# Split-precision matmuls reordered, weight remainders moved to VectorE, router logits transposed, and the mixer's per-head products issued two heads in turn

## The chip, the cores and the metric

The kernel runs on 1 core of one Trainium2 chip, written in Bass with the Tile framework. The metric is the device time of one execution in microseconds (us); a run's time is read from the device, and a profiled execution gives the trace from which every row below is taken. TensorE (PE) multiplies, VectorE (DVE) and GpSimd (POOL) work elementwise, ScalarE (ACT) casts and evaluates functions, SyncE (SP) issues the transfers of weights. Matmul results land in PSUM, which has 8 banks a partition.

## The reference

Two layers on 256 tokens of width 1024. Each layer is a token mixer with three branches (mLSTM with 4 heads, forgetting attention with 8 heads, RWKV7 with 8 heads), then cross-attention to 256 memory tokens, then a feed-forward part (dense SwiGLU in layer 0, a mixture of 8 experts with top 2 in layer 1), each closed by a residual LayerNorm.

```python
def _token_mixer(x, w_in, b_in, ...):
    p = x @ w_in + b_in
    h_a = _mlstm(m_q, m_k, m_v, col('m_i'), col('m_f'))
    ...
    h_b = _forgetting_attention(f_q, f_k, f_v, col('f_f'))
    ...
    y = _rwkv7_scan(r, decay, k, v, kk, kk * a)
    ...
    merged = gates[..., 0, :] * (h_a @ m_up) + gates[..., 1, :] * (h_b @ f_up) + gates[..., 2, :] * (y @ r_up)
    return merged @ w_out, v_own

def _moe(x, router_w, router_b, ex_wgu, ex_wd):
    logits = (x @ router_w).astype(jnp.float32) + router_b
    top_v, top_i = lax.top_k(logits, TOP_K)
    top_w = jax.nn.softmax(top_v, axis=-1)
    comb = jnp.sum(jax.nn.one_hot(top_i, N_EXPERTS, dtype=jnp.float32) * top_w[..., None], axis=-2).astype(x.dtype)
    y = jnp.zeros_like(x)
    for e in range(N_EXPERTS):
        y = y + comb[..., e:e + 1] * _swiglu(x, ex_wgu[e], ex_wd[e])
    return y

def reference(x, mem, ...):
    for l in range(DEPTH):
        mix, v_own = _token_mixer(x, *mixer_params[l], vres)
        x = _post_norm(x, mix, *ln1[l])
        x = _post_norm(x, _cross_attention(x, mem_n, *xattn[l]), *ln2[l])
        f = _swiglu(x, *ffn[l]) if l % 2 == 0 else _moe(x, *ffn[l])
        x = _post_norm(x, f, *ln3[l])
    return x
```

All inputs are fp32, and the results have to be near fp32, which sets how the kernel multiplies.

## The kernel before, in words

**Weights.** All large weights stream from HBM in 912 chunks of 512 KB (128 partitions x 1024). `chunk` (L286) transfers one to `raw` (queue of SP), ACT casts it to `whi` (L295, a rounded fp32r copy), and the remainder `wlo` = `raw` - `whi` is subtracted on DVE (L297). A list called `aside` sends 3 subtractions at the end of each `out_proj` to POOL instead, 15 in all. Activations are split in the same way into a high and a low part (`xh` and `xl`, `hh` and `hl`). `mm3` (L323) then makes one product of three fp32r matmuls at L331: `whi`·`xh`, `whi`·`xl`, `wlo`·`xh`, in that order for each of the `kt` blocks of the contraction.

**Stages.** Each layer runs `attention` (the mixer, L415), an `out_proj` (L389) with a LayerNorm, `cross` (L1056), another `out_proj`, then `dense` (L1120) in layer 0 or `moe` (L1148) in layer 1. Tile's scheduler orders the instructions of each engine by priority and dependence; every engine then runs its list in order, and PSUM tiles come from small rings by tag. In the mixer the rings are `g` (projections `fps`, 2 banks), `r` (RWKV grams and scratch, 2), `a` (scores of all three branches, 2), `p` (1) and `y` (1).

**The mixer.** `_mixer_heads` (L472) goes through a list, ORDER: projections of each branch (`fps`, 24 matmuls of 256 columns for each 128 outputs) in turn with the head work that depends on them; the projections are the filler under the head work, which has long chains through DVE, ACT and POOL.
- `_mlstm` (L653): for each head a decay bias into `mcb`, scores `msc` = K·Q (contraction over 64, so over one half of the rows of the PE array; L669, L670), then `mnm`.
- `_fox` (L709), for two heads at a time: for each head scores `flg` = q·k (64 rows; L718, L721) with the forget bias (`grow`, `cst`) and a causal mask `negts` added by matmuls into the same PSUM tile, softmax, transposes `fpt`, then `fot` = V·P (64 output columns, one column half of the array; L746, L747).
- `_rwkv_pre` (L751): the small products `rzw` and `rza` (64 rows each, L761 and L762) and, in layer 1, `rvp` (32 rows).
- `_rwkv_chain` (L847), called once for heads pairs 0 and 1 (`c0`) and once for 2 and 3 (`c1`): for each head and each of two 128-token blocks a tile `rg` of four 128x128 gram products (64 rows, L860), masked into SBUF by DVE; then an elimination chain of 15 steps through DVE and POOL that ends in the tile `ZX` (POOL, L888), which the PE product `rzz` (L894) reads.

Products with 64 rows or 64 columns use half of the array. They are plain fp32, and one of 256 columns is two records in the trace.

**The router.** `moe` makes logits `elp` (L1195) with 128 tokens of x stationary and the 16 router columns `rwp` moving, then the top 2, their positions and the gather lists with many DVE operations on tiles of 8 to 16 columns (L1200 to L1211); meanwhile POOL splits the tokens into `xth` and `xtl` (L1221). `experts` (L1283) then streams the 672 expert chunks: the big expert of each pair goes through `mm3` into `egu`, the small ones through a block of four matmuls a chunk (L1355).

Of the kernel before, what the change touches and what calls it, by code (L numbers as in the profile page):

```python
# [9 lines left out]
F32 = mybir.dt.float32  # L10
# [9 lines left out]
P = 128  # L20
# [40 lines left out]
ASIDE = 3  # L61
# [160 lines left out]
class Model:  # L222
# [10 lines left out]
    def setup(self, ip):  # L233
# [29 lines left out]
        self.negts = self.cp.tile([P, P], BF, name="negts")  # L263
# [4 lines left out]
        nc.vector.tensor_copy(self.negts, t[:, 2])  # L268
# [17 lines left out]
    def chunk(self, src, kt, n):  # L286

        nc, e = self.nc, kt * n
        pool, nraw = self._turn(0)
        raw = pool.tile([P, 1024], F32, name="raw", tag="raw", bufs=nraw)  # L290
        pool, nparts = self._turn(1)
        hi = pool.tile([P, 1024], F32R, name="whi", tag="whi", bufs=nparts)
        lo = pool.tile([P, 1024], F32R, name="wlo", tag="wlo", bufs=nparts)
        nc.sync.dma_start(raw[:, :e], src)
        nc.scalar.copy(hi[:, :e], raw[:, :e])  # L295
        eng = nc.gpsimd if self.aside and self.aside.pop(0) else nc.vector
        eng.tensor_tensor(lo[:, :e], raw[:, :e], hi[:, :e].bitcast(F32), op=OP.subtract)  # L297
        f = lambda t: t[:, :e].rearrange("p (k n) -> p k n", k=kt)
        return f(hi), f(lo)
# [23 lines left out]
    def mm3(self, ps, wh, wl, xh, xl, kt, w_stat, wsl, xsl, first=True, last=True):  # L323
# [3 lines left out]
        for k in range(kt):  # L327
            for a, b in ((wh, xh), (wh, xl), (wl, xh)):
# [60 lines left out]
    def out_proj(self, W, xs, tail, lname, xh, xl, done=None, mid=None):  # L389
# [15 lines left out]
        self.aside = [False] * (7 - tail) + [True] * ASIDE  # L405
# [247 lines left out]
    def _mlstm(self, l, qk, v1, mo, mh, ml):  # L653
        nc, wk = self.nc, self.wk
        num = wk.tile([P, 2, 4, P + 1], F32, name="mnum", tag="w4", bufs=4)
        for h in range(4):
            j, r = h // 2, slice((h % 2) * 64, (h % 2) * 64 + 64)
            cb = self.ap.tile([P, 384], F32, name="mcb", tag="a")
            sel = self._bcast('selc', h)
            nc.tensor.matmul(cb[:, 0:256], sel, self.Q, start=True, stop=False)  # L660
            nc.tensor.matmul(cb[:, 0:128], self.identb, self.negst, start=False, stop=True)
            nc.tensor.matmul(cb[:, 256:384], sel, self.Q[:, 128:256], start=True, stop=False)
            nc.tensor.matmul(cb[:, 256:384], self.identb, self.negst, start=False, stop=True)
            w = wk.tile([P, 384], F32, name="mw", tag="w15", bufs=2)
            nc.vector.tensor_scalar(w[:, 0:256], cb[:, 0:256], self.qc[:, 0, h:h + 1], 0.0, op0=OP.add, op1=OP.min)
            nc.vector.tensor_scalar(w[:, 256:384], cb[:, 256:384], self.qc[:, 1, h:h + 1], 0.0, op0=OP.add, op1=OP.min)
            nc.scalar.activation(w, w, AF.Exp)
            sc = self.ap.tile([P, 384], F32, name="msc", tag="a")
            nc.tensor.matmul(sc[:, 0:256], qk[r, 2 + j, 0:128], qk[r, j, :], start=True, stop=True)  # L669
            nc.tensor.matmul(sc[:, 256:384], qk[r, 2 + j, 128:256], qk[r, j, 128:256], start=True, stop=True)  # L670
            nc.vector.scalar_tensor_tensor(w, sc, 1.0 / 32.0, w, op0=OP.mult, op1=OP.mult)
            nm = self.ap.tile([P, 2, P + 1], F32, name="mnm", tag="a")
            nc.tensor.matmul(nm[:, 0], w[:, 0:128], v1[:, 0, h], start=True, stop=True)
            nc.tensor.matmul(nm[:, 1], w[:, 128:256], v1[:, 0, h], start=True, stop=False)
            nc.tensor.matmul(nm[:, 1], w[:, 256:384], v1[:, 1, h], start=False, stop=True)
            nc.scalar.copy(num[:, :, h], nm)
# [32 lines left out]
    def _fox(self, l, fq, fk, fv, fh, fl):  # L709
        nc, wk = self.nc, self.wk  # L710
        for j in range(4):
            pts = []
            for hh in range(2):
                h = 2 * j + hh
                r = slice(hh * 64, hh * 64 + 64)
                sel = self._bcast('self', h)
                lg = self.ap.tile([P, 384], F32, name="flg", tag="a")
                nc.tensor.matmul(lg[:, 0:128], fq[r, j, 0:128], fk[r, j, 0:128], start=True, stop=False)  # L718
                nc.tensor.matmul(lg[:, 0:128], sel, self.Q[:, 0:128], start=False, stop=False)
                nc.tensor.matmul(lg[:, 0:128], self.identb, self.negts, start=False, stop=True)  # L720
                nc.tensor.matmul(lg[:, 128:384], fq[r, j, 128:256], fk[r, j, :], start=True, stop=False)  # L721
                nc.tensor.matmul(lg[:, 128:384], sel, self.Q, start=False, stop=False)
                nc.tensor.matmul(lg[:, 256:384], self.identb, self.negts, start=False, stop=True)
# [12 lines left out]
                nc.vector.tensor_scalar(p[:, 128:384], p[:, 128:384], sm[:, 3:4], None, op0=OP.mult)  # L736
                pt = self.ap.tile([P, 384], F32, name="fpt", tag="a")
                for i in range(3):
                    nc.tensor.transpose(pt[:, i * P:(i + 1) * P], p[:, i * P:(i + 1) * P], self.ident)
                ptb = wk.tile([P, 384], F32, name="fptb", bufs=2)  # L740
                nc.scalar.copy(ptb, pt)
                pts.append(ptb)
            ot = self.ap.tile([P, S], F32, name="fot", tag="a")
            for hh in range(2):
                r, d = slice(hh * 64, hh * 64 + 64), slice(j * P + hh * 64, j * P + hh * 64 + 64)
                nc.tensor.matmul(ot[r, :], fv[:, 0, d], pts[hh][:, 0:256], start=True, stop=False)  # L746
                nc.tensor.matmul(ot[r, 128:256], fv[:, 1, d], pts[hh][:, 256:384], start=False, stop=True)  # L747
# [3 lines left out]
    def _rwkv_pre(self, l, j, x, v_first):  # L751
# [8 lines left out]
        za = pp.tile([P, S], F32, name="rza", tag="p")  # L760
# [86 lines left out]
    def _rwkv_chain(self, l, pairs, yfull):  # L847
# [6 lines left out]
        for j, (KR, BX, vt, bon, lm) in pairs:  # L854
            for hh in range(2):
                q = slice(hh * 64, hh * 64 + 64)
                for c in range(2):
                    g = rp.tile([P, 4, P], F32, name="rg", tag="r")
                    for b in range(2):
                        nc.tensor.matmul(g[:, 2 * b:2 * b + 2].rearrange("p a b -> p (a b)"), BX[q, c, b],  # L860
                                         KR[q, c].rearrange("p a b -> p (a b)"), start=True, stop=True)
                    m = self.grams[len(M)]
                    nc.vector.copy_predicated(m, self.keep.rearrange("p a b -> p (a b)"),
                                              g.rearrange("p a b -> p (a b)"))
                    M.append(m.rearrange("p (a b) -> p a b", a=4))
# [282 lines left out]
    def moe(self, l, xh, xl):  # L1148
        tc, nc, A = self.tc, self.nc, self.A
        xt = self.xt  # L1150
        with ExitStack() as ctx:
# [37 lines left out]
            pos = wk.tile([P, 2, NE], F32, name="epos")  # L1189
            pp = tp.tile([P, 5, NE], F32, name="epp", tag="t")  # L1190
            for tt in range(2):
                lp = self.gp.tile([P, 2, NE], F32, name="elp", tag="g")
                for k in range(KD):
                    for part in (xh, xl):
                        nc.tensor.matmul(lp.rearrange("p a b -> p (a b)"), part[:, k, tt * P:(tt + 1) * P],  # L1195
                                         rwp[:, k].rearrange("p a b -> p (a b)"), start=k == 0 and part is xh,
                                         stop=k == KD - 1 and part is xl)
                nc.vector.tensor_tensor(lg[:, tt], lp[:, 0], rb, op=OP.add)
                nc.vector.tensor_tensor(lg[:, tt], lg[:, tt], lp[:, 1], op=OP.add)
                nc.vector.max(mx[:, tt], lg[:, tt])  # L1200
                nc.vector.max_index(ix[:, tt], mx[:, tt], lg[:, tt])
                nc.vector.tensor_copy(ixf[:, tt], ix[:, tt])
# [303 lines left out]
```

## Time and profile before

| what | value |
|---|---|
| runs of the kernel | 2164.92, 2165.76 (median), 2166.17 us |
| profiled execution, its own time | 2165.97 us |
| its span in the trace | 2164.2 us |
| mean granted TensorE clock | 0.987 |
| PE busy | 2082.1 us, 96% of the span, 11726 matmul records |
| DVE, ACT, POOL busy | 1601.9, 1222.3, 227.6 us |
| HBM moved | 532.18 MB, 246 GB/s over the span |

The profiled execution is within 0.21 us of the median of the runs, and 1.8 us of its time lie outside its span. "Busy" counts a matmul from its start to its modelled end, so an engine that is shown as busy may still lose time between starts: pace has to be read from start to start. The stages lie in the span as follows: mixer of layer 0 to about 345 us, mixer of layer 1 from about 700 to 1060 us, last LayerNorm and router 1179 to 1214 us, experts 1214 to 2130 us.

### The profile page before, as it was taken

What the parts mean: (1) busy time and instruction counts of PE and PEld (TensorE: products, weight loads), DVE (VectorE), ACT (ScalarE), POOL (GpSimd) and SP (SyncE); (2) the same over time, 40 slices, a digit from 0 to 9 for tenths busy, and PEclk for the clock granted to TensorE, in tenths of its full rate; (3) what the DMA queues carried; (4) which work ended last, traced back from release to release, by engine and by line L of the source; (5) the groups of instructions that cost most, each with busy time, mean ns of one, the idle gap of its engine ahead of it and who ended that gap; (6) DMA issues with size and microseconds to landing.
All of it is one profiled execution on the core that took longest, in us unless ns stands there. A gap on an engine that the chain in (4) does not pass through costs nothing.

```text
span 2164.2 us, 33290 instructions
## 1 busy us (share of the span) xinstructions
PE 2082.1 (96%) x11726; PEld 1724.1 (80%) x11726; DVE 1601.9 (74%) x2327; ACT 1222.3 (56%) x1723; POOL 227.6 (11%) x332
## 2 busy tenths in 40 slices
PE   7999999999999899999998899999999999999996
PEld 6988898989998788889887777777767767777674
DVE  6776656746555677665675698889888988899887
ACT  5443334544443544332453587777777777777774
POOL 0031142202001113114212100000000000000000
PEclk9999999999999999999999799999999999999998
DMA  5431335645553543133574599999999999999994
GB/s 199 157 120 59 135 123 200 253 151 202 189 185 124 173 152 111 62 104 111 214 263 146 179 366 393 389 363 363 388 388 363 372 386 385 391 354 372 379 393 181
DMA packets 146767, 532.18 MB, mean 246 GB/s; under 512 B 16672, under 2 KB 17184, under 8 KB 145568
## 3 DMA queue, kind: packets, MB, share of 16 engines
q1 hardware_dynamic: 142128, 520.16, 64.9%
q10 hardware_dynamic: 4080, 8.77, 1.2%
q8 instruction: 94, 1.54, 0.3%
q0 software_dynamic: 384, 1.05, 0.1%
q14 instruction: 81, 0.66, 0.1%
HBM read 525.19 MB, written 4.72 MB: 245 GB/s over the span
## 4 chain that ended last, share of the span: by engine, by line
PE 52%; DMA 12%; DVE 10%; issue 3%; ACT 2%; POOL 1%; SPq 0%; DVEq 0%; ACTq 0%; POOLq 0%
DVE wlo L297 8%; DMA raw<-in_ex_wgu 7%; PE fps L331 7%; PE ops L331 6%; PE dps L331 6%; PE xps L331 5%; DMA raw<-in_ex_wd 5%; PE eacc L1372 4%; PE egu L331 4%; PE egu L1355 4%; PE eacc L331 2%; PE eacc L1379 2%; PE ups L331 2%; ACT whi L295 2%; PE eg L1315 1%
## 5 line engine op out<-in xcount | busy, mean ns | idle before, releaser
L297 DVE TENSOR_TENSOR wlo<-raw,whi 128x1024 fp32r<-128x1024 f32 x897 | 1073.9, 1231 | 261.4 <-ACT whi L295 251.5
L295 ACT CAST whi<-raw 128x1024 fp32r<-128x1024 f32 x912 | 916.2, 1049 | 468.0 <-PE fps L331 159.8
L331 PE MATMUL fps<-xh,whi 128*128 128x256 f32 x816 | 238.6, 293 | 7.5 <-ACT cu L543 4.9
L331 PE MATMUL fps<-xl,whi 128*128 128x256 f32 x816 | 235.0, 288 | 3.2 <-DVE xl L336 3.2
L331 PE MATMUL fps<-xh,wlo 128*128 128x256 f32 x816 | 236.4, 290 | 0.2
L1355 PE MATMUL egu<-wlo,xgs 128*128 128x512 f32 x448 | 198.1, 443 | 12.2 <-DVE wlo L297 12.2
L331 PE MATMUL egu<-wlo,xgh 128*128 128x512 f32 x448 | 178.9, 401 | 2.7 <-DVE wlo L297 2.6
L331 PE MATMUL egu<-whi,xgh 128*128 128x512 f32 x448 | 179.1, 401 | 0.8 <-ACT esl L1390 0.8
L331 PE MATMUL egu<-whi,xgl 128*128 128x512 f32 x448 | 178.2, 398 | 0.0
L1355 PE MATMUL egu<-whi,xgs 128*128 128x512 f32 x448 | 178.0, 398 | 0.0
L331 PEld LDWEIGHTS fps<-xh,whi 128*128 128x128 f32 x816 | 156.1, 191 | 13.9 <-ACT cu L543 5.7
L331 PEld LDWEIGHTS fps<-xl,whi 128*128 128x128 f32 x816 | 156.0, 191 | 5.7 <-DVE xl L336 3.5
L331 PEld LDWEIGHTS fps<-xh,wlo 128*128 128x128 f32 x816 | 156.0, 191 | 3.0 <-issue 2.0
L364 POOL TENSOR_TENSOR lnve<-lnve,mhalf 128x1 f32<-128x1 f32 x14 | 14.5, 1038 | 1282.2 <-DVE lnve L363 1282.2
L1355 PEld LDWEIGHTS egu<-wlo,xgs 128*128 128x128 f32 x448 | 84.0, 188 | 74.8 <-DVE wlo L297 60.9
L331 PE MATMUL eacc<-whi,ehl 128*128 128x512 f32 x448 | 124.6, 395 | 0.0
L331 PEld LDWEIGHTS egu<-wlo,xgh 128*128 128x128 f32 x448 | 84.7, 189 | 26.9 <-DVE wlo L297 7.8
L1372 PE MATMUL eacc<-raw,ehf 128*128 128x512 f32 x224 | 104.8, 594 | 0.1
L331 PEld LDWEIGHTS egu<-whi,xgl 128*128 128x128 f32 x448 | 84.8, 189 | 20.2 <-issue 0.7
L331 PEld LDWEIGHTS egu<-whi,xgh 128*128 128x128 f32 x448 | 84.5, 189 | 20.0 <-ACT esl L1390 1.0
L331 PEld LDWEIGHTS eacc<-whi,ehl 128*128 128x128 f32 x448 | 83.8, 188 | 20.0 <-DVE ehl L336 0.2
L331 PE MATMUL dps<-xl,whi 128*128 128x256 f32 x352 | 98.9, 281 | 0.6 <-DVE xl L336 0.6
(427 smaller groups left out, 4048.2 us busy)
## 6 DMA issues: line engine op xcount, KB each, us to landing
raw<-in_ex_wgu SPq DMA_DIRECT2D x448, 512.0 KB, 6.0
raw<-in_ex_wd SPq DMA_DIRECT2D x224, 512.0 KB, 5.8
raw<-in_w_fm SPq DMA_DIRECT2D x54, 512.0 KB, 3.3
raw<-in_w_gate SPq DMA_DIRECT2D x48, 512.0 KB, 3.2
raw<-in_ff_wgu SPq DMA_DIRECT2D x44, 512.0 KB, 4.3
raw<-in_w_tm SPq DMA_DIRECT2D x24, 512.0 KB, 3.3
raw<-in_ff_wd SPq DMA_DIRECT2D x22, 512.0 KB, 4.3
raw<-in_w_out SPq DMA_DIRECT2D x16, 512.0 KB, 3.9
```

Of the source, the lines that this page charges most:

```text
L295: nc.scalar.copy(hi[:, :e], raw[:, :e])
L297: eng.tensor_tensor(lo[:, :e], raw[:, :e], hi[:, :e].bitcast(F32), op=OP.subtract)
L331: nc.tensor.matmul(ps, l, r, start=first and n == 0, stop=last and n == 3 * kt - 1)
L364: nc.gpsimd.tensor_tensor(ve[:, 1:2], ve[:, 0:1], self.mhalf[:, 0:1], op=OP.pow)
L1315: nc.tensor.matmul(ps[:, kk, :n * P], src[:, tt, o], pb[:, tt, lo:hi].rearrange("p a b -> p (a b)"), start=tt == 0, stop=tt == 1)
L1355: nc.tensor.matmul(ps, x[2][:, 2 * q + kk], part[:, kk], start=q + kk + n == 0, stop=q == 3 and kk == 1 and n == 1)
L1372: nc.tensor.matmul(acc[h], ht[0][:, i], w[:, h * 512:(h + 1) * 512], start=f, stop=l)
L1379: nc.tensor.matmul(acc[h], ht[1][:, i - 2].rearrange("p a b -> p (a b)"), part[:, 0, s], start=f and n == 0, stop=l and n == 1)
```

## The change

1. `mm3` and the block of the small expert run through the contraction once for each kind of product: all `whi` products first, those with `wlo` last.
2. `aside` is gone: all 912 `wlo` subtractions are on DVE.
3. The router's logits are transposed (`elt`: 16 router columns stationary, 128 tokens moving), copied by ACT (`els`) and brought back by one small matmul with `fold`; the small DVE operations of both token halves are joined; the `xtl` subtractions go from POOL to DVE.
4. In the mixer the products of two heads are issued in turn, so that neighbours use different halves of the array and different PSUM banks: `msc` and `flg` of two heads, `fot` in turn, the grams `rg` of two heads of a pair (two tiles of ring `r` at once); `rza` moves from ring `p` to ring `a`, so that `rzw` and `rza` have a bank each. In `_fox` the mask `negts` is widened to 384 columns and opens the accumulation once a head.

```diff
         nc = self.nc
         n = 0
-        for k in range(kt):
-            for a, b in ((wh, xh), (wh, xl), (wl, xh)):
+        for a, b in ((wh, xh), (wh, xl), (wl, xh)):
+            for k in range(kt):
                 w, x = a[:, k, wsl], b[:, k, xsl]
...
-        eng = nc.gpsimd if self.aside and self.aside.pop(0) else nc.vector
-        eng.tensor_tensor(lo[:, :e], raw[:, :e], hi[:, :e].bitcast(F32), op=OP.subtract)
+        nc.vector.tensor_tensor(lo[:, :e], raw[:, :e], hi[:, :e].bitcast(F32), op=OP.subtract)
...
+            scs = [self.ap.tile([P, 384], F32, name="msc", tag="a") for _ in range(2)]
+            for o, t, q in ((slice(0, 256), slice(0, 128), slice(0, 256)), (slice(256, 384), slice(128, 256), slice(128, 256))):
+                for hh, sc in enumerate(scs):
+                    r = slice(hh * 64, hh * 64 + 64)
+                    nc.tensor.matmul(sc[:, o], qk[r, 2 + j, t], qk[r, j, q], start=True, stop=True)
...
+            lgs = [self.ap.tile([P, 384], F32, name="flg", tag="a") for _ in range(2)]
+            for lg in lgs:
+                nc.tensor.matmul(lg, self.identb, self.negts, start=True, stop=False)
+            for o, t, n in ((slice(0, 128), slice(0, 128), 128), (slice(128, 384), slice(128, 256), 256)):
+                for hh, lg in enumerate(lgs):
+                    r = slice(hh * 64, hh * 64 + 64)
+                    nc.tensor.matmul(lg[:, o], fq[r, j, t], fk[r, j, :n], start=False, stop=False)
...
+            for tt, o in enumerate((slice(0, 256), slice(128, 256))):
+                for hh in range(2):
+                    r, d = slice(hh * 64, hh * 64 + 64), slice(j * P + hh * 64, j * P + hh * 64 + 64)
+                    nc.tensor.matmul(ot[r, o], fv[:, tt, d], pts[hh][:, 256 * tt:256 + 128 * tt], start=tt == 0,
+                                     stop=tt == 1)
...
-        za = pp.tile([P, S], F32, name="rza", tag="p")
+        za = self.ap.tile([P, S], F32, name="rza", tag="a")
...
-            for hh in range(2):
-                q = slice(hh * 64, hh * 64 + 64)
-                for c in range(2):
-                    g = rp.tile([P, 4, P], F32, name="rg", tag="r")
-                    for b in range(2):
+            for c in range(2):
+
+                gs = [rp.tile([P, 4, P], F32, name="rg", tag="r") for _ in range(2)]
+                for b in range(2):
+                    for hh, g in enumerate(gs):
+                        q = slice(hh * 64, hh * 64 + 64)
                         nc.tensor.matmul(g[:, 2 * b:2 * b + 2].rearrange("p a b -> p (a b)"), BX[q, c, b],
                                          KR[q, c].rearrange("p a b -> p (a b)"), start=True, stop=True)
...
-                lp = self.gp.tile([P, 2, NE], F32, name="elp", tag="g")
+                lt = self.gp.tile([2 * NE, P], F32, name="elt", tag="g")
                 for k in range(KD):
                     for part in (xh, xl):
-                        nc.tensor.matmul(lp.rearrange("p a b -> p (a b)"), part[:, k, tt * P:(tt + 1) * P],
-                                         rwp[:, k].rearrange("p a b -> p (a b)"), start=k == 0 and part is xh,
-                                         stop=k == KD - 1 and part is xl)
...
+                        nc.tensor.matmul(lt, rwp[:, k].rearrange("p a b -> p (a b)"), part[:, k, tt * P:(tt + 1) * P],
+                                         start=k == 0 and part is xh, stop=k == KD - 1 and part is xl)
+                ls = wk.tile([2 * NE, P], F32, name="els", bufs=2)
+                nc.scalar.copy(ls, lt)
+                nc.tensor.matmul(pp[:, 3 + tt], ls, fold, start=True, stop=True)
...
-                    nc.gpsimd.tensor_tensor(tl[o], xt[o], th[o].bitcast(F32), op=OP.subtract)
+            for h in range(2):
+                for tt in range(2):
+                    o = (slice(None), tt, slice(h * 512, (h + 1) * 512))
+                    nc.vector.tensor_tensor(tl[o], xt[o], th[o].bitcast(F32), op=OP.subtract)
```

The scheduler decides what in fact stands side by side. On PE, in the forgetting attention of layer 0, before (one head: its 128-column and its 256-column score product, each followed by its bias and mask; `grow` and `cst` make the bias, `identb` and `negts` the mask):

```order
L739 MATMUL fpt<-ident,fp 128x128 x3
L718 MATMUL flg<-fk,fq 128x128
L719 MATMUL flg<-grow,cst 128x128
L720 LDWEIGHTS identb
L720 MATMUL flg<-negts,identb 128x128
L721 MATMUL flg<-fk,fq 128x256
L722 MATMUL flg<-grow,cst 128x256
L723 LDWEIGHTS identb
L723 MATMUL flg<-negts,identb 128x128
L761 MATMUL rzw<-mm,wa 128x256
```

The same place on PE in the changed kernel (the four grams of two heads and `rzw`, then the second of the two `flg` tiles):

```order
L871 MATMUL rg<-KR,BX 128x256 x4
L770 MATMUL rzw<-mm,wa 128x256
L755 MATMUL fot<-fptb,fv 64x256 x2
L720 LDWEIGHTS identb
L720 MATMUL flg<-negts,identb 128x384
L724 MATMUL flg<-fk,fq 128x128
L724 MATMUL flg<-fk,fq 128x256
L727 MATMUL flg<-grow,cst 128x128
L728 MATMUL flg<-grow,cst 128x256
L331 MATMUL fps<-xh,whi 128x256
L755 MATMUL fot<-fptb,fv 64x128 x2
```

Both score products of a head now stand together, so that a head makes one stretch in half-array products where it made two; but most heads still stand alone, since the second `flg` tile comes free later than the first. The two `fot` products of 256 columns stand together, one for each head.

On PE, the grams of the second chain (`c1`) of layer 0, before:

```order
L331 MATMUL fps<-xh,whi 128x256
L860 MATMUL rg<-KR,BX 128x256 x2
L331 MATMUL fps<-xl,whi 128x256
L331 MATMUL fps<-xh,wlo 128x256
L860 MATMUL rg<-KR,BX 128x256 x2
L331 MATMUL fps<-xh,whi 128x256
```

And in the changed kernel:

```order
L331 MATMUL fps<-xh,whi 128x256 x2
L871 MATMUL rg<-KR,BX 128x256 x2
L331 MATMUL fps<-xh,whi 128x256 x6
L331 MATMUL fps<-xl,whi 128x256 x8
L331 MATMUL fps<-xh,wlo 128x256 x3
L871 MATMUL rg<-KR,BX 128x256 x2
```

In this chain each group of two still belongs to one head, as before; in the first chains most groups hold both heads.

On DVE, the last LayerNorm of layer 1 ahead of the router, before (`lnr` is the residual, `lnst` and `lnmv` its moments, `lnve` what POOL raises to the power -1/2; `rwp` is the split router weight):

```order
L385 SCALAR_TENSOR_TENSOR lnr<-xt,ops 128x512
L359 BN_STATS lnst<-lnr 128x6
L363 TENSOR_SCALAR lnve<-lnmv 128x1
L373 SCALAR_TENSOR_TENSOR xt<-lnr,lnmv,lngb 128x512 x2
L359 BN_STATS lnst<-lnr 128x6
L297 TENSOR_TENSOR wlo<-raw,whi 128x1024
L336 TENSOR_TENSOR rwp<-rw,rwp 128x8x8
L361 BN_AGGR lnmv<-lnst 128x2
```

And in the changed kernel:

```order
L385 SCALAR_TENSOR_TENSOR lnr<-xt,ops 128x512
L359 BN_STATS lnst<-lnr 128x6
L297 TENSOR_TENSOR wlo<-raw,whi 128x1024
L361 BN_AGGR lnmv<-lnst 128x2
L297 TENSOR_TENSOR wlo<-raw,whi 128x1024
L359 BN_STATS lnst<-lnr 128x6
L336 TENSOR_TENSOR rwp<-rw,rwp 128x8x8
L363 TENSOR_SCALAR lnve<-lnmv 128x1
L373 SCALAR_TENSOR_TENSOR xt<-lnr,lnmv,lngb 128x512 x2
```

Two subtractions of 1024 columns that POOL made now stand on DVE ahead of the `lnve` that the whole stage goes through.

## Rows read from the trace of the kernel before

**Rows 1.** The page, part 4: chain that ended last, shares of the span by engine.
```profile
PE 52%; DMA 12%; DVE 10%; issue 3%; ACT 2%; POOL 1%; SPq 0%; DVEq 0%; ACTq 0%; POOLq 0%
```

**Rows 2.** Windows: length, busy us of PE, PEld, DVE, ACT, POOL; PEclk, DMA, GB/s.
```profile
20.00:350.00 330.00, 324.66 (x2344) 291.26 (x2343) 216.72 (x512) 140.55 (x257) 69.81 (x122) 1.00 0.36 123
705.00:1060.00 355.00, 344.57 (x2460) 309.38 (x2460) 226.43 (x532) 146.26 (x264) 73.40 (x136) 0.99 0.35 117
1180.00:1214.00 34.00, 21.59 (x87) 19.83 (x88) 24.52 (x70) 8.18 (x16) 12.46 (x14) 0.55 0.37 141
1214.00:1260.00 46.00, 45.19 (x226) 37.54 (x225) 37.21 (x35) 38.81 (x52) 0.00 (x0) 1.00 0.79 272
1260.00:2130.00 870.00, 852.86 (x3544) 627.74 (x3544) 775.23 (x785) 657.15 (x825) 0.00 (x0) 1.00 0.99 380
```

**Rows 3.** Timeline of PE, layer 1's mixer: start, length, line, tile, shape, count.
```profile
808.01 0.28 PE L331 MATMUL fps<-xh,wlo 128*128 128x256 f32 x1
808.13 0.29 PE L331 MATMUL fps<-xh,whi 128*128 128x256 f32 x1
808.35 1.13 PE L860 MATMUL rg<-KR,BX 64*128 64x256 f32 x4
809.40 0.39 PE L331 MATMUL fps<-xl,whi 128*128 128x256 f32 x1
```

**Rows 4.** Timeline of PE, layer 0's mixer, grams beside rzw.
```profile
109.28 0.48 PE L860 MATMUL rg<-KR,BX 64*128 64x256 f32 x1
109.29 0.48 PE L761 MATMUL rzw<-mm,wa 64*128 64x256 f32 x1
109.60 0.38 PE L860 MATMUL rg<-KR,BX 64*128 64x256 f32 x1
109.61 0.38 PE L761 MATMUL rzw<-mm,wa 64*128 64x256 f32 x1
109.81 0.59 PE L860 MATMUL rg<-KR,BX 64*128 64x256 f32 x2
110.34 0.39 PE L331 MATMUL fps<-xh,whi 128*128 128x256 f32 x1
```

**Rows 5.** Groups by line on PE, shapes apart: records, busy us, mean ns, idle before.
```profile
L860 PE MATMUL rg<-KR,BX 64*128 64x256 f32 x128 | 35.3, 400 | 0.0
L721 PE MATMUL flg<-fk,fq 64*128 64x256 f32 x32 | 11.1, 428 | 0.0
L746 PE MATMUL fot<-fptb,fv 128*64 128x256 f32 x32 | 10.3, 405 | 0.0
L718 PE MATMUL flg<-fk,fq 64*128 64x128 f32 x32 | 7.8, 322 | 0.0
```

**Rows 6.** Waits of PE: waiting line, releaser, total us, count, mean us.
```profile
PE rzz L894 <- POOL ZX L888: 5.8, 2, 2.9
```

**Rows 7.** Timeline of DVE, POOL and PE around the LayerNorm before the router.
```profile
1179.83 2.35 POOL L297 TENSOR_TENSOR wlo<-raw,whi 128x1024 fp32r<-128x1024 f32 x1
1180.79 0.14 DVE L363 TENSOR_SCALAR lnve<-lnmv 128x1 f32<-128x1 f32 x1
1183.91 1.63 POOL L364 TENSOR_TENSOR lnve<-lnve,mhalf 128x1 f32<-128x1 f32 x1
1186.47 1.94 PE L343 MATMUL tp<-ident,xt 128*128 128x128 f32 x8 [6.93 <-DVE xt L374]
```

**Rows 8.** Timeline of POOL and DVE in the router.
```profile
1198.56 5.04 POOL L1221 TENSOR_TENSOR xtl<-xt,xth 128x512 fp32r<-128x512 f32 x4 [6.89 <-ACT xth L1220]
1202.45 1.32 DVE L1204 TENSOR_SCALAR eoh<-eit,eixf 128x8 f32<-128x8 f32 x2
1205.08 0.17 DVE L1211 TENSOR_SCALAR epos<-epos 128x8 f32<-128x8 f32 x1
```

**Rows 9.** The page, part 5: the remainder on DVE.
```profile
L297 DVE TENSOR_TENSOR wlo<-raw,whi 128x1024 fp32r<-128x1024 f32 x897 | 1073.9, 1231 | 261.4 <-ACT whi L295 251.5
```

**Rows 10.** Waits in the experts: waiting line, releaser, total us, count, mean us.
```profile
PEld egu L1355 <- DVE wlo L297: 60.9, 140, 1.1
```

More of the change, by code (lines that the diff above doesn't have):

```diff
@@ L60 @@
 AHEAD = 2000
-ASIDE = 3
 FIRST = 65536.0
@@ L262, in setup @@
         self.negst = self.cp.tile([P, P], BF, name="negst")
-        self.negts = self.cp.tile([P, P], BF, name="negts")
+        self.negts = self.cp.tile([P, 3 * P], BF, name="negts")
+        nc.gpsimd.memset(self.negts, 0.0)
         self.keep = self.cp.tile([P, 4, P], U8, name="keep")
@@ L267, in setup @@
         nc.vector.tensor_copy(self.negst, t[:, 1])
-        nc.vector.tensor_copy(self.negts, t[:, 2])
+        for i in (0, 2):
+            nc.vector.tensor_copy(self.negts[:, i * P:(i + 1) * P], t[:, 2])
         for i in range(4):
@@ L655, in _mlstm @@
         num = wk.tile([P, 2, 4, P + 1], F32, name="mnum", tag="w4", bufs=4)
[L656 to L676, printed above, removed]
@@ L711, in _fox @@
         for j in range(4):
-            pts = []
-            for hh in range(2):
[L714 to L723, printed above, removed]
+            lgs = [self.ap.tile([P, 384], F32, name="flg", tag="a") for _ in range(2)]
[5 more added lines that the diff above has]
+                    nc.tensor.matmul(lg[:, o], fq[r, j, t], fk[r, j, :n], start=False, stop=False)
+            for hh, lg in enumerate(lgs):
+                sel = self._bcast('self', 2 * j + hh)
+                nc.tensor.matmul(lg[:, 0:128], sel, self.Q[:, 0:128], start=False, stop=False)
+                nc.tensor.matmul(lg[:, 128:384], sel, self.Q, start=False, stop=True)
+            pts = []
+            for lg in lgs:
                 m = self.stat.tile([P, 6], F32, name="fm")
@@ L1352, in block @@
                         continue
-                    for kk in range(2):
-                        for n, part in enumerate((wh, wl)):
+                    for n, part in enumerate((wh, wl)):
+                        for kk in range(2):
                             nc.tensor.matmul(ps, x[2][:, 2 * q + kk], part[:, kk], start=q + kk + n == 0,
@@ L1475, in run @@
                     self.to_fm(self.tp, xt[:, tt], xh, xl, tt, h)
-        self.rings, self.aside, self.used, self.count = [], [], {}, 0
+        self.rings, self.used, self.count = [], {}, 0
         self.stream(self.ctx, 3, 3)
```

64 lines of the change are left out of this document (42 added, 22 removed).

## The prediction

> **What bounds the kernel now.** I read the chain of waits first. TensorE holds 52% of the chain that ended last, DMA 12% and VectorE 10% [rows 1], so no single answer holds for the whole span, and each part of the change has to be priced in its own stage. The windows show three kinds of stage [rows 2]. In the two mixers TensorE is busy for 324.66 of 330.00 and 344.57 of 355.00 us at the full granted clock while DMA stands at 0.36 and 0.35: whatever shortens TensorE's own list shortens the mixer. Around the last LayerNorm and the router TensorE is busy for 21.59 of 34.00 us at a granted clock of 0.55: there the end is set by chains of short operations on VectorE and GpSimd. In the experts DMA is at 0.79 for 46 us and then at 0.99 for 870 us: TensorE is busy too (852.86 us), but the transfers come one after the other without a gap, and little can be won.
>
> What "busy" hides is seen in the timeline of TensorE. `fps` matmuls of 256 columns start 0.12 us apart (808.01, 808.13). Between the `fps` ahead of four gram records and the `fps` behind them lie 1.27 us [rows 3]. Four records of half the array take about 0.216 us each, (1.13 - 0.48) / 3, so 4 x 0.216 + 0.12 = 0.98 us are accounted for, and 0.29 us are not. I take that as the cost of going into the half-array form and back. I went through the records of both mixers for every such excursion: there are 104, the median cost is 0.295 us, and the one shown is typical; together some 30 us.
>
> **The change part by part.**
>
> *Fewer excursions.* By the order of the changed kernel the mixers make 79 excursions instead of 104: `rg` 29 to 27, `flg` 32 to 17 (both products of a head now stand together), `fot` 22 to 17, `msc` 8 to 6, `rza` 8 to 7. 25 x 0.29 = **-7.2 us**. Ends: 0 (if the 0.29 us belongs to each change of the half, not to each stretch) and -7.4.
>
> *Two halves at once.* Half-array products of 256 columns come to 248 records: `rg` 128, `flg` 32, `fot` 32 [rows 5], and `rzw`, `rza`, `msc` with 16 each and `rvp` with 8. At 0.216 us they take 53.6 us; 80 more of 128 columns (`flg` 32 [rows 5], `fot` 32, `msc` 16) at half of that add 8.7 us, 62 us in all. Whether two halves run at once is shown in a single place: a gram on one half and `rzw` on the other start at 109.28 and 109.29, and again at 109.60 and 109.61 [rows 4]. Six records of 0.216 us, 1.30 us in a row, took from 109.28 to 110.34, less 0.2 us for the way back about 0.85 us: four slots instead of six. I walked the changed order, letting neighbours on different halves run side by side. Because the scheduler has pulled most pairs apart (the second gram chain of each layer still goes two records of one head, then fillers; most `flg` stand alone), 53.0 us remain of 61.9, **-8.9 us**. Of it 2.6 us come from the column halves of `fot`, which no row shows together. Ends: 0 and -8.9.
>
> The Trainium skill (TensorE: Matmul & The Clock Gate, Part 3, The mechanism) says that matmuls start and end in program order, without reordering. By that rule both records of the first head would go before the first of the second, the overlap would be one record shorter in every such place, and the walk gives 55.8 us instead of 53.0. The row contradicts it here: `rzw`'s first record started at 109.29, ahead of the second gram record at 109.60 [rows 4].
>
> *Wider mask.* `negts` now covers 384 columns a head instead of twice 128: 16 heads x 128 columns at half of 0.12 us [rows 3]: **+1.0 us**.
>
> *The RWKV chain.* TensorE waits 2.9 us for `ZX` in the second chain of each layer [rows 6]: there the work that covers the chain through VectorE and GpSimd is used up, so it counts what lies between the last gram and the first `rzz`. By both orders and 0.12 us an `fps` this filler goes from 19.3 to 17.4 us in layer 0 and from 19.1 to 19.9 in layer 1, so those two waits change by +1.9 and -0.8. In the first chains it falls from 23.4 to 21.8 and from 22.6 to 19.7 us; there is no wait today, and the cover becomes about as long as the chain. Sum **+2 us**, ends 0 and +5.
>
> *Remainders on VectorE, and the router.* `aside` was there to spare VectorE, but at the last LayerNorm it blocks GpSimd: `lnve` was ready at 1180.79 + 0.14, its power on GpSimd began at 1183.91, behind a subtraction of 2.35 us that began at 1179.83, and TensorE waited 6.93 us for `xt` [rows 7]. In the changed order two subtractions stand on VectorE ahead of `lnve`, 1.23 us each [rows 9]. What GpSimd's queue gives back (3.0 us from ready to start) VectorE takes (2.5 us): about 0 there. In the router VectorE's tiny operations take 1.15 to 1.32 us where the same kind takes 0.17 (1202.45 for one pair against 1205.08), and all those long ones lie inside GpSimd's `xtl` of 5.04 us from 1198.56 [rows 8]. With `xtl` gone from GpSimd I take -4 us; its four subtractions on VectorE, about half of 1.23 us each, cost +2.5 us, of which some 1 us stands in VectorE's idle time. The transposed logits need as many products, one copy on ACT and a small product more a token half, but bring half of the matmul's latency at the low clock: 0 +-2. Sum **-2.5 us**, ends -6 and +2. At the other four LayerNorms a subtraction moved to VectorE lies beside products of the same weights: 0 +-3.
>
> *The order of the products.* In the mixer and cross-attention the same matmuls run in another order: 0. In the experts it brings the remainder's deadline later: the weight loads of `egu` wait 60.9 us for `wlo` in 140 places [rows 10]. But they stand beside DMA at 0.99. The most that can be won is what DMA leaves free: 0.21 x 46 + 0.01 x 870 = 18 us [rows 2]. With nothing that makes the first 46 us fetch faster except earlier release of buffers, I take **-3 us**, ends 0 and -18.
>
> Sum: -7.2 - 8.9 + 1.0 + 2 - 2.5 - 3 = -18.6 us. The profiled execution took 2165.97 us (span 2164.2 and 1.8 around it), 0.2 us over the median of the runs: 2165.97 - 18.6 = **2147 us**.
>
> **The rivals.**
> - *The experts give more.* Later deadlines for `wlo` release the buffers evenly and DMA fills its gaps: 15 us more, 2132 us. For it: 60.9 us of waits for `wlo`. Against it: DMA at 0.99.
> - *The halves don't run together,* because the weights of the second product have to be loaded behind the first. No row shows two heads of one branch side by side. Then the 8.9 us stay: 2156 us.
> - *Program order,* as the skill's rule in the part on halves has it: two records of one head go first, then two of the other. 2.8 us of the 8.9 are lost: 2150 us.
> - *Slower.* Ring `a` has two banks, and now both are held by two heads together in 12 places (8 in `_fox`, 4 in `_mlstm`), and `rza` takes one as well. TensorE works its list in order; if at each place it waits for VectorE or ACT to free the second bank as long as it does for `ZX` (2.9 us [rows 6]), that is +35 us and the time 2182 us. Today there is no idle time ahead of `flg` [rows 5], and in the changed order `fps` stand between the tiles. It decides the sign from 18.6 / 12 = 1.6 us a place on.
> - *Nothing is won.* The mixer isn't bound by TensorE's list but by the chains that its head work hangs on; what TensorE saves comes back as longer waits for `ZX` and `wlo`: 2163 to 2169 us. Against it: TensorE's 0.98 in the mixer.
>
> **How the numbers follow.** The forecast 0.58, with its own range from the ends of its terms (0.29 us not won in a third of the places, chain +5, router and LayerNorms +-4) of 2140 to 2154; program order 0.05; no overlap 0.11; experts 0.10; slower 0.09; nothing won 0.07. A range of 2131 to 2160 takes in the first three and most of the fourth, and leaves out about 0.2. A measurement of this kernel can tell about 0.2%, 4.3 us, from no change, so faster means below 2161.4: 0.58 + 0.05 + 0.11 + 0.10 = 0.84 and no more; the same 0.07; slower 0.09.
>
> **What the profile after will show.** If the steps hold: the mixer of layer 0 ends about 7 us earlier and that of layer 1 about 14 us earlier in all; TensorE's records of two halves start 0.01 us apart where two heads stand together; the wait of `rzz` for `ZX` stays between 2 and 5 us each; long tiny operations on VectorE in the router are gone; the experts take as long as before within 5 us. The prediction is wrong if TensorE shows new idle time ahead of `flg`, `fpt` or `msc` (slower), if records of different halves never start together (no overlap), if the saved time stands again ahead of `rzz` or `wlo` (nothing won), or if the window of 870 us shrinks by 10 or more (experts).

## The result, and the profile after

The changed kernel takes 2149.75 us (median of 4 runs, 2145.81 to 2151.66) against 2165.97 us before on the same chip (median of 4, 2164.92 to 2166.67): a ratio of 0.9918, 95% interval 0.9900 to 0.9937, or 16.2 us less. The forecast was 2147. The profiled execution was the slowest of the four (2151.66 us, span 2149.6 us).

The windows of the changed kernel, in the columns and stretches of [rows 2] (the changed program is a few us ahead in them):

```profile
20.00:350.00 330.00, 318.97 (x2350) 289.27 (x2349) 217.38 (x514) 142.89 (x258) 73.07 (x122) 0.99 0.38 125
705.00:1060.00 355.00, 340.82 (x2434) 307.38 (x2433) 226.57 (x530) 147.52 (x261) 72.65 (x132) 0.97 0.34 116
1180.00:1214.00 34.00, 21.75 (x109) 19.29 (x110) 21.81 (x67) 10.54 (x21) 2.96 (x4) 0.65 0.38 137
1214.00:1260.00 46.00, 44.93 (x219) 36.80 (x218) 38.80 (x36) 38.88 (x53) 0.00 (x0) 1.00 0.85 288
1260.00:2130.00 870.00, 855.99 (x3579) 634.74 (x3578) 782.61 (x794) 658.60 (x829) 0.00 (x0) 1.00 0.98 379
```

The mixers now have a little more idle TensorE time and a granted clock of 0.99 and 0.97 instead of 1.00 and 0.99. The experts look as before; yet most of the gain is there. Part of the reason is that the last window holds 13 us behind the last transfer now. The same 621 chunks, from the landing of the 51st of the experts' 672 to that of the last, before and changed:

```profile
1271.94:2131.09 859.15, 841.47 (x3493) 618.17 (x3491) 764.58 (x774) 647.81 (x813) 0.00 (x0) 1.00 0.99 380
1267.83:2116.70 848.87, 835.27 (x3502) 620.79 (x3500) 765.06 (x775) 647.27 (x815) 0.00 (x0) 1.00 0.99 384
```

They took 10.3 us less, at the same shown share of busy DMA engines. To see where the rest lies, I cut TensorE's list of both traces at the first start of each stage's own matmuls (`fps`, `ops`, `dps`; for the experts at the first and last `egu`, for the router at the last `ops`). In each stage I added up what the records take at the pace of undisturbed ones (0.119 us for 256 columns of `fps`, 0.232 for 512 columns, 0.213 for a record of a half-array product), what the stretches in half-array products take beyond or under that, and the rest, which is waits and clock. (In the router the transposed logits, 16 columns wide, count as such stretches now; what is left of a difference beside these two is work.) `clock` is the part of the rest that the granted clock explains (1 minus the clock, times its length).

```
us                    before                              changed              difference
              wall  stretches  rest  clock       wall  stretches  rest  clock
mixer 0     352.76     16.39  20.29   0.00     348.35      7.11  24.78   1.71    -4.41
out + cross 146.32      0      3.50   0.00     147.28      0      4.46   0.11    +0.96
dense       201.28      0      1.21   0.00     200.79      0      1.14   1.60    -0.50
mixer 1     354.31     19.44  18.82   3.41     357.28     12.59  27.82  10.24    +2.97
out + cross 113.63      0      7.05   3.41     113.24      0      6.66   1.71    -0.39
LN, router   29.09      0     21.27  12.68      27.56      6.38  13.20   9.91    -1.54
experts     928.66      0     95.97   2.68     916.89      0     84.20   2.04   -11.77
```

With 0.1 us at the start and the end this is the whole difference of the spans, 2164.2 - 2149.6 = 14.6 us. Two things stand out. The stretches became 16.1 us cheaper, 35.83 to 19.70, which is what the two terms on pairing say (-7.2 - 8.9); but the rest of the mixers grew by 13.5 us, and their work by 1.2 us (the wider mask), so that they gave 1.4 us in all. And the experts gave 11.8 us, where -3 was forecast; 3.8 us of it is idle time of TensorE (18.5 to 14.7), most of the rest lies between starts of matmuls that are shown as busy.

The pairing does what it says. In the timeline of TensorE, changed kernel (start, length, line, tile, shape, count):

```profile
107.82 0.34 PE L720 MATMUL flg<-negts,identb 128*128 128x384 bf16 x1
108.09 1.14 PE L871 MATMUL rg<-KR,BX 64*128 64x256 f32 x8
109.16 0.34 PE L720 MATMUL flg<-negts,identb 128*128 128x384 bf16 x1
...
140.29 0.65 PE L755 MATMUL fot<-fptb,fv 128*64 128x256 f32 x4
...
176.28 0.65 PE L755 MATMUL fot<-fptb,fv 128*64 128x256 f32 x2
```

Eight gram records of two heads take 1.14 us, where four of one head took 1.13 [rows 3]. Four `fot` records of two heads take as long (0.65 us) as two of one head: column halves, for which no row stood ahead, run side by side as well.

What took it back is in the waits of the changed kernel (line, releaser, total us, count, longest; the last number of [rows 6] and [rows 10] is the longest wait too, not the mean):

```profile
PE rzz L905 <- POOL ZX L899: 8.2, 5, 2.9
PE tp L640 <- DVE grow L637: 4.9, 2, 2.9
PE ups L331 <- ACT hTh L335: 3.3, 2, 1.7
PE tp L343 <- DVE xt L374: 11.0, 2, 8.8
PEld egu L1374 <- DVE wlo L297: 52.0, 113, 1.0
```

And two of the kernel before:

```profile
PE fps L331 <- ACT cu L543: 4.9, 2, 3.1
PE ups L331 <- ACT hTh L335: 1.8, 2, 0.9
```

The wait for `ZX`, 5.8 us in 2 places [rows 6], is 8.2 us in 5. The one ahead of the transposes of `grow` is new by name only: it stands where `fps` waited 4.9 us for `cu`. In all, TensorE's idle time in the mixers grew by 3.2 us in layer 0 (11.0 to 14.2) and by 4.1 in layer 1 (10.6 to 14.7), and what the clock takes by 1.7 and 6.8 us. That is 7.3 + 8.5 = 15.8 us, where the rest grew by 13.5: the two don't add up exactly, since the ends of matmuls are modelled and idle time at the lower clock counts in both.

One of the new waits costs more than its length; TensorE's timeline, and the windows just before and behind:

```profile
869.46 0.50 PE L799 MATMUL rss<-cst,rdc 128*128 128x2 f32 x4
871.67 1.30 PE L905 MATMUL rzz<-ident,ZX 128*128 128x128 f32 x3 [1.71 <-POOL ZX L899]
```

```profile
865.00:871.50 6.50, 4.96 (x43) 4.87 (x42) 6.09 (x20) 4.72 (x11) 5.56 (x13) 1.00 0.45 163
871.50:878.40 6.90, 6.73 (x29) 6.00 (x30) 1.35 (x5) 1.52 (x3) 4.61 (x10) 0.51 0.22 78
```

Behind a wait of 1.71 us for `ZX` the granted clock is 0.51 for 6.90 us (1.2 instead of 2.4 GHz), in which TensorE works 6.73 us: about 3.4 us lost on top of the wait. Before, there was no wait at this chain, and the clock stayed up:

```profile
871.00:878.00 7.00, 7.00 (x57) 6.16 (x56) 5.80 (x13) 3.81 (x10) 0.66 (x2) 1.00 0.40 138
```

Not every wait does this: in layer 0 one of 2.2 us for `ZX` and one of 2.9 us for `grow` cost no clock. The other half of layer 1's new clock loss is in part a matter of where the stage ends. It stands at 1049.05 to 1055.87, behind a wait of 1.5 us for `hTh`; before, a stretch as long began at 1066.83, 1.3 us behind the mixer's end, and is counted in the next stage. Taken together, the mixer of layer 1 and the stage behind it lost 6.8 us to the clock before and 12.0 us after.

### The profile page after: what moved, and what is told of

It is laid out like the page before. It is cut to its first block, busy times and chain, and to the rows that moved or that the text cites. A ratio compares the mean times of both kernels' runs of the same rounds, so it can differ in the third digit from the quotient of the medians.

```text
span 2149.6 us, 33258 instructions
## 1 busy us (share of the span) xinstructions
PE 2062.3 (96%) x11714; PEld 1719.1 (80%) x11714; DVE 1598.5 (74%) x2339; ACT 1227.3 (57%) x1725; POOL 183.1 (9%) x315
## 4 chain that ended last, share of the span: by engine, by line
PE 65%; DMA 13%; DVE 12%; issue 4%; ACT 4%; POOL 2%; SPq 0%; DVEq 0%; POOLq 0%; ACTq 0%
PE fps L331 14%; DVE wlo L297 8%; DMA raw<-in_ex_wgu 7%; PE ops L331 7%; PE xps L331 6%; PE dps L331 6%; PE egu L331 5%; DMA raw<-in_ex_wd 5%; PE egu L1374 4%; PE eacc L1391 3%; PE ups L331 3%; ACT whi L296 3%; PE eacc L331 2%; PE rg L871 1%; PE eacc L1398 1%
## 5 line engine op out<-in xcount | busy, mean ns | idle before, releaser
L331 PE MATMUL egu<-whi,xgh 128*128 128x512 f32 x448 | 142.3, 399 | 0.8 <-ACT esl L1409 0.8
L1374 PE MATMUL egu<-whi,xgs 128*128 128x512 f32 x448 | 141.1, 397 | 0.7 <-ACT whi L296 0.7
L331 PE MATMUL egu<-wlo,xgh 128*128 128x512 f32 x448 | 141.0, 398 | 0.0
L331 PE MATMUL fps<-xh,whi 128*128 128x256 f32 x816 | 125.9, 293 | 4.4 <-ACT xh L335 1.6
L331 PE MATMUL fps<-xl,whi 128*128 128x256 f32 x816 | 127.0, 290 | 2.0 <-DVE xl L336 2.0
L331 PE MATMUL fps<-xh,wlo 128*128 128x256 f32 x816 | 124.1, 289 | 0.0
L331 PEld LDWEIGHTS fps<-xh,whi 128*128 128x128 f32 x816 | 108.0, 192 | 11.7 <-issue 2.5
L331 PEld LDWEIGHTS fps<-xl,whi 128*128 128x128 f32 x816 | 108.8, 191 | 6.0 <-issue 3.4
L331 PEld LDWEIGHTS fps<-xh,wlo 128*128 128x128 f32 x816 | 107.6, 190 | 4.0 <-issue 3.4
L1374 PEld LDWEIGHTS egu<-whi,xgs 128*128 128x128 f32 x448 | 83.5, 188 | 21.2 <-ACT whi L296 2.2
```

The costliest lines, as they stand in the source:

```text
L331: nc.tensor.matmul(ps, l, r, start=first and n == 0, stop=last and n == 3 * kt - 1)
L1374: nc.tensor.matmul(ps, x[2][:, 2 * q + kk], part[:, kk], start=q + kk + n == 0, stop=q == 3 and kk == 1 and n == 1)
```

## The experiments

All times below are against runs of the kernel before on the same chip (its medians were 2166.2, 2167.9 and 2167.9 us in the three sets); stage numbers are from the same account as above. The scatter of a stage has to be kept in mind: `e3`, `e7` and `e8` leave the mixers' instructions as before, and layer 0's mixer took 353.96, 350.85 and 350.69 us in them beside 352.76 before. Its clock loss was 3.41 us in e3 and none in the other three. A difference of 2 us in one stage says little by itself; layer 1's mixer was steadier (354.06, 354.37, 354.35 us, clock loss 3.41 us in all). Cross-attention is counted from its first product to the end of its stage. In layer 1 it took 1.8 and 1.7 us more in `e7` and `e8` than before (0.2 in `e3`), and the `out_proj` ahead of it 2.9 us less, though these leave both as they were.

**e1_heads: the pairing alone** (`_mlstm`, `_fox`, `rza`, grams, wide mask; `mm3`, `aside` and the router as before).

> The kernel before with the two-heads-in-turn part alone (_mlstm, _fox, rza, the grams, the wide mask). My account of the changed kernel's trace: against before, the half-array stretches of the two mixers cost 16.1 us less (35.8 to 19.7 us), and waits and clock drops in the mixers took 14.6 us back. Theory A (the pairing itself makes the waits: each PSUM ring is held by two heads, the fillers are pulled from the chains): -1 to -4 us here, stretches still 14 to 17 us cheaper, and the waits there. Rival B (the other order of the products in mm3 makes the waits): -12 to -17 us here, since mm3 is as before. The experts, 928.7 us from their first to their last egu, should stay within 2 us in either.

Measured 2157.29 us, ratio 0.9952 (0.9939 to 0.9966), -8.9 us by the point, between the two theories. The stretches are 16.6 us cheaper (8.61 and 10.65), the rest of the mixers 6.4 us dearer, 4.5 of it in layer 1; the experts take 928.86 us, as before. So in these traces the pairing itself brings about half of what the waits and the clock took in the whole change (6.4 of 13.5).

**e2_order: the order of the products alone.**

```diff
-        for k in range(kt):
-            for a, b in ((wh, xh), (wh, xl), (wl, xh)):
+        for a, b in ((wh, xh), (wh, xl), (wl, xh)):
+            for k in range(kt):
...
-                    for kk in range(2):
-                        for n, part in enumerate((wh, wl)):
+                    for n, part in enumerate((wh, wl)):
+                        for kk in range(2):
```

> The kernel before with the order of the products alone (mm3 and the small expert's block). Theory A: the experts take 10 to 13 us less and the mixers stay within 3 us: -8 to -13 us. Rival B: the experts as in A, but the mixers 8 to 14 us longer by waits: -3 to +3 us. Rival C (the experts' 11.8 us of the changed kernel were another rate of the transfers in that execution, not the order): 0 to +-3 us with the experts unchanged.

Measured 2161.05 us, ratio 0.9980 (0.9970 to 0.9990). The experts are 12.7 us shorter (915.98), so rival C falls. The mixers are 1.3 us shorter and their idle time 2.9 us less, so the order alone makes no new waits there in all, against rival B (the waits for `ZX` rose from 5.8 to 7.1 us, others fell). But both cross-attentions are longer, by 2.6 and 3.8 us. The trace is that of the fastest of nine runs (2156.65 us), 4.4 us under their median, so that its stages show less of the loss than the time does.

**e3_expert_order: the late `wlo` in the experts alone** (the same order for `egu` and the small block; a flag leaves the other calls of `mm3` as before).

> The kernel before with the late wlo only in the experts (mm3 of egu and the small block); the rest of mm3 as before. Theory A: -10 to -13 us, all between the first and the last egu. Rival C: 0 to +-3 us. If B holds for e2, this one is 8 to 14 us faster than e2.

Measured 2154.56 us, ratio 0.9945 (0.9932 to 0.9959), -11.7 us; the experts 12.6 us shorter (916.05). It is as theory A expected, and by the medians some 6 us better than the order everywhere.

**e4_lists: all remainders on VectorE and the router, alone.**

> The kernel before with the two other parts (all remainders on VectorE; the router transposed, its small operations joined and xtl on VectorE). By the account of the changed kernel the stage from the last ops to the first egu took 1.5 us less there, and LayerNorm stages in between +2: 0 +-3 us in every theory; more than 4 us either way would say that these parts move the order elsewhere.

Measured 2169.62 us, ratio 1.0010 (1.0001 to 1.0019). The LayerNorm and router stage is 1.2 us shorter, cross-attention 2.6 us longer in layer 0 (the 1.4 us in layer 1 are no more than `e7` and `e8` show): alone these parts cost a little, 3.4 us by the medians with an interval that ends next to nothing.

**e5_heads_expert: e1 and e3 together.**

> The kernel before with two parts alone: the two heads in turn, and the late wlo in the experts only (e1 and e3 together). Theory A (the two gains lie in different stages and add; the rest of the change costs): -8.9 - 11.7 = -20 us, so -18 to -23, and 3 to 5 us faster than the whole change (2149.75). Rival B (the parts that cost alone belong to the sum, as the whole change measured 5 us better than its parts added up): -14 to -17 us, no better than the whole change.

Measured 2146.17 us, ratio 0.9901 (0.9887 to 0.9916), -21.7 us: the two gains add, theory A. The difference to the whole change (0.9918) goes the expected way, but the two intervals overlap.

**e6_order_noaside: e2 with all remainders on VectorE.** In e2 GpSimd's three subtractions run while VectorE applies the LayerNorm; the timeline of e2 there:

```profile
390.19 8.12 POOL L297 TENSOR_TENSOR wlo<-raw,whi 128x1024 fp32r<-128x1024 f32 x3
390.99 2.29 DVE L374 SCALAR_TENSOR_TENSOR xt<-xt,lnve,lngb 128x512 f32<-128x512 f32 x1
393.20 0.68 DVE L385 SCALAR_TENSOR_TENSOR lnr<-xt,ops 128x512 f32<-128x512 f32 x1
393.80 2.26 DVE L374 SCALAR_TENSOR_TENSOR xt<-xt,lnve,lngb 128x512 f32<-128x512 f32 x1
396.12 0.66 PE L343 MATMUL tp<-ident,xt 128*128 128x128 f32 x4 [1.15 <-DVE xt L374]
```

And before, where both operations start ahead of GpSimd's first subtraction (at 389.09):

```profile
388.37 1.39 DVE L374 SCALAR_TENSOR_TENSOR xt<-xt,lnve,lngb 128x512 f32<-128x512 f32 x2
```

> e2 (the order of the products everywhere) with all remainders on VectorE. In e2 cross-attention took 6.4 us more, in idle time ahead of the transposes tp, while GpSimd made subtractions beside VectorE's xt operations (2.29 us instead of 0.70). Theory A (the new order moves the LayerNorm's VectorE operations beside GpSimd's subtractions, and the collision is what costs): without GpSimd's subtractions cross-attention returns to within 2 us of before, and the time is 4 to 6 us under e2, at -9 to -11. Rival B (the order alone puts the transposes where x isn't ready): cross-attention stays 4 us or more over before, -2 to -6.

Measured 2160.03 us, ratio 0.9964 (0.9951 to 0.9976), -7.9 us: between the two theories, and its interval overlaps that of `e2`. Cross-attention returned to +0.7 us in layer 0, as theory A says, and to +2.2 in layer 1, of which `e7` and `e8` show 1.7 to 1.8 without any change there; the mixer of layer 0 was 5.5 us longer in the profiled execution. The collision is there to be read in e2, and it goes away without `aside`; that it is the whole of the loss isn't shown.

**e7_big and e8_small: the late `wlo` in one kind of expert.**

> The kernel before with the late wlo in the big experts' egu alone (six matmuls a chunk). Theory A (TensorE is nearly full in a big expert's part, and there it waited for wlo: its time lost ahead of big egu products falls from 12.2 us of before to 4.5 in the whole change): -8 to -12 us. Rival B (the small expert's 60.9 us of waits of the weight loads are what counts): 0 to -3 us.

> The kernel before with the late wlo in the small experts' block alone (four matmuls a chunk). Theory A: 0 to -3 us, since there TensorE waits for the transfers in any order. Rival B: -8 to -12 us.

e7 took 2157.91 us, ratio 0.9960 (0.9948 to 0.9972), the experts 7.8 us shorter; e8 2163.96 us, ratio 0.9984 (0.9975 to 0.9993), the experts 3.1 us shorter. Together 10.9 of the 12.6 us. TensorE's loads of big-expert `wlo` (busy us, mean ns, idle before, releaser), first in e8, which leaves the big experts as before, then in the changed kernel:

```profile
L331 PEld LDWEIGHTS egu<-wlo,xgh 128*128 128x128 f32 x448 | 84.7, 189 | 27.4 <-DVE wlo L297 8.3
```

```profile
L331 PEld LDWEIGHTS egu<-wlo,xgh 128*128 128x128 f32 x448 | 83.2, 188 | 19.3
```

8.3 us of waits for `wlo` are gone. The small experts' waits, 60.9 us in 140 places [rows 10], which looked like the larger part, fell only to 52.0.

**e9_rg_expert and e10_scores_expert: e3 with half of the pairing each** (`_rwkv_chain` alone; `_mlstm`, `_fox` and `_rwkv_pre` alone).

> The kernel before with the late wlo in the experts (worth -12 us in e3) and only the grams of two heads in turn. By its order 99 half-array stretches instead of 104, and some 3 us of records side by side: 4 to 5 us cheaper stretches. Theory A (what TensorE saves ahead of the RWKV chains comes back in the wait for ZX): -11 to -14 us, the stretches 4 to 5 us cheaper and the waits of rzz for ZX up by 2 or more. Rival B (the gram pairs are kept in full): -16 to -17 us.

> The kernel before with the late wlo in the experts and the score products of two heads in turn (_mlstm, _fox, rza), the grams as before. By its order 79 stretches instead of 104 and some 3 us side by side: 10 to 12 us cheaper stretches. Theory A: most of the 9 us that the pairing is worth is here, 4 to 5 us come back as waits for ZX: -17 to -20 us. Rival B (kept in full): -22 to -24 us. If neither e9 nor this one reaches e5 (-21.7), both halves of the pairing are needed.

e9 took 2156.02 us, ratio 0.9943 (0.9927 to 0.9959), no better than e3; e10 2148.63 us, ratio 0.9912 (0.9899 to 0.9924). The stretches are 5.1 us cheaper in e9 and 10.8 in e10, together 15.9, near the 16.6 of e1. Both times are where theory A put them, and in both the rest of the mixers grew by 5.65 us. In e10 the waits for `ZX` went from 5.8 to 7.7 us, as A says. In e9 they were 3.2 us, less than before, while the clock loss in the mixers went from 3.41 to 10.24 us: there A's mechanism is not what ate the gain. Two new waits of `fps` for `wlo` in layer 0 (2.0 and 2.6 us) each stand ahead of a stretch at half clock; the scatter of layer 0 may be part of it as well. The profiled execution of e10 (2155.11 us) is the slowest of its five and has 5.9 us more in layer 1's cross-attention, whose code wasn't changed.

**e12b_parts4: the old order with deeper `whi` and `wlo` rings.**

```diff
-RAWS = 6
+RAWS = 4
...
-            self.ring(ctx, [self.rawp, RAWS])
+            self.ring(ctx, [self.rawp, RAWS], [self.rawp, 1])
```

> The kernel before, product order as before, with a fourth pair of whi and wlo buffers in the experts (and 4 further raw buffers instead of 6, which pays for their place). Theory A (the late wlo helps because TensorE meets it later; buffers are not short): the experts 0 to 6 us longer by the missing raw buffers, none shorter. Rival B (the order helps because a whi buffer is free earlier, so ACT casts and the transfers' buffers turn faster): the experts 4 to 12 us shorter with the old order.

Measured 2169.58 us, ratio 1.0015 (1.0006 to 1.0024), the experts +0.5 us. A fourth buffer doesn't bring what the order brings, so theory A is left, by elimination; that two missing raw buffers hid a small gain can't be excluded. How an earlier finish of TensorE makes the transfers come sooner, no run shows step by step.

**e13_after_expert: the changed kernel, with the new order in the experts alone.**

> The changed kernel with its new product order in the experts alone (so e5 and the two other parts: all remainders on VectorE, the router). If those two parts cost 3 us as they did alone (e4: +3.4), this one is at -17 to -19 us, as the whole change (2149.75 beside 2165.97). If the order outside the experts is what the whole change loses against e5, it is at -21 to -23.

Measured 2145.64 us, ratio 0.9895 (0.9881 to 0.9910), -22.3 us, the fastest version by the point. Beside e5 the two list parts cost nothing, although they cost 3.4 us alone; by the medians, the 5.5 to 6 us that the whole change loses against e5 and e13 come with the new order outside the experts, in layer 1's mixer by the traces (357.28 us against 350.33 and 352.71; clock loss 10.24 us against 5.12 and 6.83). The intervals of the whole change and of these two overlap a little.

## Why the forecast was right in its time and wrong in its parts

- **Fewer excursions and two halves at once** (-7.2 and -8.9): 16.1 us of cheaper stretches measured, 16.6 in e1. Right in mechanism and size. The rival of program order falls with it: if both records of a head had to start ahead of the other head's, eight gram records would fill five slots (0, 1 and 1, 2 and 2, 3 and 3, 4), about 0.22 us more than the 1.14 us that they took. The Trainium skill (TensorE: Matmul & The Clock Gate, Part 3, The mechanism) has matmuls start and end in program order; the trace doesn't agree for the two records of such a product.
- **The wider mask** (+1.0): the work of the mixers grew by 1.2 us in the account. Right.
- **The RWKV chain** (+2): right for the wait that it prices and in its sum (the waits for `ZX` rose by 2.4 us), not in its places: the second chain of layer 0 waits 2.8 us where 4.8 was expected, that of layer 1 2.9 us where 2.1 was, and 0.8 and 1.7 us are new in the two first chains. The step that failed is that nothing else was priced: the sum has no term for the other waits of the mixers (`hTh`, `lw`, `yn` and more; idle time +7.3 us with `ZX`) and none for the clock, which it takes as full. The clock took 8.5 us more in the mixers; counted with the stages behind them, as above, layer 1's share of this is 5.1 us instead of 6.8. Its loss in layer 1's mixer was 3.41 us in `before`, e3, e7, e8 and e12b, but 5.12 in e2 and e4, whose mixers have no pairs either, so it isn't the pairing alone that moves it. The rival that nothing is won was right for the mixers: they gave 1.4 us of 16.1.
- **The order of the products** (-3, ends 0 and -18): the mechanism was named, the size was wrong by four. The 11.8 us lie inside the ends, but the step "little can be won", since the transfers come without a gap, failed. The 621 chunks took 10.3 us less, where a free share of 0.01 leaves 9 in all. By the transfers' records the share rose only from 0.990 to 0.995, some 4.5 us; so the rest has to come from transfers that took less time themselves. The share of busy DMA engines doesn't say that they run at their rate. In the changed kernel from 1300 to 1400 us, in 40 slices of 2.5 us:

```profile
DMA  9999999999999999998999999999999999999999
GB/s 410 411 408 413 410 405 406 411 406 411 388 344 372 390 408 406 362 346 234 362 415 416 413 418 406 405 411 405 398 416 370 338 393 416 415 410 403 406 387 393
```

  Engines that are shown as busy move 234 to 418 GB/s. I took the times at which the chunks land: half of them follow the one before by 1.279 us or less, in both kernels, but the mean over the 621 chunks is 1.383 us before and 1.367 after. If every chunk came at the pace of the median, (1.383 - 1.279) x 621 = 65 us would be won, an estimate that no run reaches; 10 us of it were.
- **Router and LayerNorm** (-2.5): -1.5 measured. The stage lost 9.9 us to the clock instead of 12.7, so that without the clock it would be 1.2 us longer, not shorter; the term had no such step. The forms of operation came out as said: the joined `eoh` pair takes 0.26 us where one pair took 1.32 [rows 8]; but the longest wait of the transposes for `xt` rose from 6.93 [rows 7] to 8.8 us, with the two subtractions ahead on VectorE. The transposed logits, set at 0, take 7.0 us from the first product to the last, where `elp` took 9.4.
- **The rivals.** The slower one (waits at the two banks of ring `a`) didn't come: the trace after shows no idle time ahead of `flg`, and 0.4 us ahead of `fot`. "The experts give more" was right to 9 of its 15 us, and its sign, a window shorter by 10 us or more, came true. The total came out near the likeliest case by luck: a gain put four times too small (3 us for 11.8 in the experts) and a loss put five times too small (3 us for 14.7 in the mixers) cancelled.

## What to carry to other kernels

A DMA share near 1 doesn't say that a stream runs at its best rate: compare the rate with the best rate of the same stream, slice by slice. What an engine saves in front of a chain that another engine sets can come back as a wait, and a wait can cost the clock behind it too, as the one of 1.71 us did here. A reordering that helps one stage can cost in another: try it by stage; here the order was worth 12 us in the experts and cost some 6 us elsewhere, by the medians.

## What the hardware showed that was not expected

Column halves (`fot`, two heads in 0.65 us as one) overlap as row halves do. VectorE's `xt` operation of 128 x 512 at L374, with `xt` and `lngb` as inputs, took 2.26 to 2.29 us beside GpSimd's subtractions and 0.70 to 0.75 without; the one at L385 that reads `ops` from PSUM took 0.68 us beside them. Going into and out of a stretch in half-array products costs 0.29 us in the changed kernel too (median of its stretches), whether one head's products stand in it (0.296) or two (0.31, 8 stretches behind an `fps`).
